# Layer two's phase of values: three tiles kept in DRAM during it, and the transposes for the queries issued beside the third value chunk

## The chip, the core and the metric

The kernel runs on one core of a Trainium2 chip. The metric is the device time of one execution in microseconds (us). Three runs of the kernel before took 2206.42, 2208.21 and 2209.02 us; their median is 2208.21 us. A separate execution was recorded by the hardware profiler: it took 2207.9 us on the device, and its trace spans 2206.1 us, so 1.8 us lie around the span. Every duration below comes from that one recorded execution.

## What is computed

A decoder trunk of two layers on 256 positions of width 2048, all in float32. Layer one mixes tokens by dilated attention and by attention into 256 memory tokens, and then runs a gated MLP with a short convolution. Layer two takes keys and values (`k_sh`, `v_sh`, 12 heads of 128) from the normed output of layer one, queries from its own norm, and mixes by stick-breaking attention and by 4-head attention into the memory tokens; the same kind of MLP follows.

```python
kv = _rmsnorm(x, g_kv) @ w_kv
k_sh, v_sh = jnp.split(kv, 2, axis=-1)
h = _rmsnorm(x, nrm[0])
q, qm = jnp.split(h @ w_in_b[lb], [SB_W], axis=-1)
o_sb = _stick_breaking(q.reshape(B, S, SB_HEADS, HEAD_DIM), k_sh, v_sh)
o_mem = _memory_attention(qm, mem, nrm[4], w_mem_kv[layer])   # mk, mv = rmsnorm(mem) @ w_mem_kv
x = _finish_layer(x, jnp.concatenate([o_sb.reshape(B, S, -1), o_mem], -1), ...)
```

## The kernel before

Nearly all of the time is matrix multiplication. Each float32 operand is split into a high part (`whi`, cast on ACT, line 629) and a low part (`wlo`, subtracted on DVE, line 630), and a product is made of three matmuls (`mm3`, line 127), or of a wider pair in `ws_tile` and `ws_beside`. Weights come in pieces of 1 MB or 768 KB into `raw`, which has three buffers, on SP's queue: the load of a piece waits until the piece three loads earlier has been split.

**The stage that the change touches.** After layer one's MLP, `run` goes through these steps, and the names are those of the profile:

- `mem_v(1)` has just made `mv`, the memory values (line 524 evacuates them); `mk`, the memory keys, was made long before, while layer one's output projection ran, and lies in its buffer through the whole MLP of layer one.
- `v_proj` (line 1159, `as_chunk`) makes `v2`, the third chunk of 512 values, from four pieces of weights. Each piece begins with `self.step()`, which runs whatever `later(units, fn)` has put there for that unit.
- `x_T` (lines 273 to 284) makes the transposed input of the queries: 32 transposes on PE (line 280) into PSUM, then 16 casts on ACT (269) and 16 subtractions on DVE (270) into `hq`.
- `qm_proj` makes the queries for the memory heads from `hq`, in four `ws_tile`s (lines 145 to 150).
- `values`, by way of `wide`, makes the other 1024 value columns in eight units. A unit multiplies seven half-size products instead of eight, over sums of the weights and sums of the input; beside it, `ws_beside` (lines 156 to 176) makes one tile of the keys. Everything in it is pinned, that is, it stays on each engine in the order in which the code writes it. The same routine runs in layer one (there beside tiles of queries and keys) and in the MLPs.

**What a unit u of `wide` loads and does.** `first_sums` brings `d` for unit u + 2: a 512 KB load on SP's queue (636), then an accumulating load of 512 KB on POOL's queue (637) into the same tile. `load` brings `raw` of unit u + 1 (668, 768 KB), and `ws_beside` the key weights of unit u + 1 (156, 1 MB). On SP's queue they stand in this order, so `raw` and the key weights wait behind `d`. DVE then makes the sums `e` from `d` and `raw` (674, 675), splits `raw` and the key weights, and splits `d` and `e` into the tiles `forms` (`x<-sh`, 630).

**The buffers.** `d` and `e` take buffers of the tag `sh`, of 512 KB each, of which there are 11. Through the phase of values eight are taken: `mk`, `mv`, `v2`, `qm` and the four places of `sums_of_h(hk, 4)`. Three are left, for two `d` and one `e`. So `d` of unit u + 2 goes where `d` of unit u lies, and its load waits for the split of that tile on DVE. In layer one's phase the sums of the input lie in a set of their own, and the waiting tiles are fewer: six `sh` buffers are left there.

Outside `wide` a scheduler sets each engine's order from the order of the code and from what is ready.

Of the kernel before, what the change touches and what calls it, by code (L numbers as in the profile page):

```python
# [10 lines left out]
F32 = mybir.dt.float32  # L11
# [6 lines left out]
P = 128  # L18
# [12 lines left out]
COL_G = {"a0": 0, "a2": 16, "a4": 32, "b0": 48, "b2": 64, "b4": 80, "kv": 96}  # L31
# [14 lines left out]
class Body:  # L46
# [49 lines left out]
    def pin(self, ins):  # L96
        return self.tc.keep_in_program_order(ins) if self.pinned else ins
# [291 lines left out]

    def dil_head(self, h, q, k, V, hi, lo, when):  # L390


        st = {}
        self.later(when[0], lambda: self.dil_scores(q, k, st))
        self.later(when[1], lambda: self.dil_turn(st))
        self.later(when[2], lambda: self.dil_out(h, V, st, hi, lo))

# [41 lines left out]

    def dil_out(self, h, V, st, hi, lo):  # L440
        nc = self.nc
        p0, p1 = st["p"]
        o = self.bank("s")
        hs = slice(h * E, (h + 1) * E)
        for g in range(3):
            nc.tensor.matmul(o[:, 0:P], V[g][:, 0, hs], p0[:, g, :], start=g == 0, stop=g == 2)
        for g in range(3):
            for kb in range(2):
                nc.tensor.matmul(o[:, P:S], V[g][:, kb, hs], p1[:, 2 * g + kb, :],
                                 start=g == 0 and kb == 0, stop=g == 2 and kb == 1)  # L450
        self.split_heads(o[:, :S], hi, lo)


    def sb_pair(self, j, q, k, V, outs, first):

        st = {}
        self.later(first, lambda: self.sb_scores(q, k, st))
        self.later(first + 3, lambda: self.sb_turn(st))
        self.later(first + 4, lambda: self.sb_out(j, V, st, outs))
# [85 lines left out]
    def out_proj(self, layer, src, lhs, each, filler=None):  # L545
# [39 lines left out]
        else:  # L585
            self.add_normed(ys, r[1], 1, each)

    def sums_of_h(self, h, ring=0):

        nc, pin = self.nc, self.pin
        if ring:
            places = [self.sh([P, 4, 2, P], F32R) for _ in range(ring)]
            room = lambda: self.sc([P, 2, S])
        else:
            whole = self.sb.tile([P, KT // 2, 4, 2, P], F32R, name="h1", tag="h1", bufs=1)
            places = [whole[:, i] for i in range(KT // 2)]
            room = self.pairtile  # L600
        s = lambda u: places[u % len(places)]

        def less(out, x, y):

            pin(nc.vector.scalar_tensor_tensor(out, x, -1.0, y, op0=ALU.mult, op1=ALU.subtract))

        def make(i):
            a, d = room(), room().rearrange("p a (b t) -> p (a b) t", b=2)
            hh = h[2][:, 2 * i:2 * i + 2, :, :].bitcast(F32)
            pin(nc.vector.tensor_add(a, hh[:, :, 0, :], hh[:, :, 1, :]))  # L610
            a1, a2 = a[:, :, 0:P], a[:, :, P:S]
            pin(nc.vector.tensor_sub(d[:, 0, :], a2[:, 1, :], a2[:, 0, :]))
            less(d[:, 1, :], d[:, 0, :], a1[:, 0, :])
            pin(nc.vector.tensor_sub(d[:, 2, :], a1[:, 0, :], a2[:, 0, :]))
            less(d[:, 3, :], d[:, 1, :], a1[:, 1, :])
            return lambda: self.split_heads(d, s(i)[:, :, 0, :], s(i)[:, :, 1, :])

        return s, make
# [391 lines left out]
    def run(self):  # L1010
        nc, a = self.nc, self.a
# [52 lines left out]
        mv = self.mem_v(0, before, 17)  # L1064
        h = self.hset("h2")
        mk = self.mem_k(0, lambda j: self.load_T(a["xT"], COL_G["a0"], h, j), 13)
# [24 lines left out]
        s, make = self.sums_of_h(h)  # L1091
        for i, at in enumerate((0, 1, 2, 2, 3)):
            self.later(at, lambda i=i: make(i)())
        ahead = []
        self.later(2, lambda: ahead.extend(self.first_sums(a["wv01_a"], u) for u in range(2)))
        v2 = self.v_proj(a["wv_a"][0], h)
        qm = self.qm_proj(a["wqm_a"], h, 1)

        forms = self.sb.tile([P, 4, 1024], F32R, name="x", tag="x", bufs=1)
# [15 lines left out]
        V = self.values(a["wv01_a"], ahead, h, s, forms, tile, self.rest_of(make)) + [v2]  # L1115
# [27 lines left out]
        hk = self.hset("h2")  # L1143
# [9 lines left out]
        mk, mv = res["mk"], res["mv"]  # L1153


        with self.tc.issue_after(self.last_hi.ins):
            self.r = self.x_rstd()
        self.later(3, spread)
        v2 = self.v_proj(a["wv_b"][0], hk)
        hq = self.hset("h1")  # L1160
        self.x_T(COL_G["b0"], hq)

        for t in range(2):
            self.later(0, lambda t=t: nc.gpsimd.dma_start(self.xout[t], self.x[:, t, :]))
        s, make = self.sums_of_h(hk, 4)
        for i in range(4):
            self.later(i, lambda i=i: make(i)())
        ahead = []
        self.later(2, lambda: ahead.extend(self.first_sums(a["wv01_b"], u) for u in range(2)))
        qm = self.qm_proj(a["wqm_b"], hq)  # L1170
        forms = self.sb.tile([P, 4, 1024], F32R, name="x", tag="x", bufs=1)
# [14 lines left out]
        def begin(i):  # L1186
            halves[i] = make(i)


        also = {0: lambda: begin(4), 1: lambda: halves[4](), 2: lambda: begin(5), 3: lambda: halves[5](),  # L1190
                4: lambda: (begin(6), halves[6]()), 5: lambda: begin(7), 6: lambda: halves[7]()}
        V = self.values(a["wv01_b"], ahead, hk, s, forms, tile, also) + [v2]
        self.x = sb.tile([P, 2, D], F32, name="x", tag="x", bufs=1)
        for t in range(2):
            self.later(8 + t, lambda t=t: nc.gpsimd.dma_start(self.x[:, t, :], self.xout[t]))
# [131 lines left out]
```

## Time and profile before

| | |
|---|---|
| median of three runs | 2208.21 us |
| profiled execution: time, span of the trace | 2207.9 us, 2206.1 us |
| mean granted TensorE clock over the span | 0.996 |
| instructions on PE, DVE, ACT, POOL | 10926, 2348, 1896, 195 |
| HBM read and written | 508.60 MB, 25.17 MB |
| phase of values in layer one, in the trace | from 98.7 to 182.5 us |
| `v_proj`, `qm_proj`, phase of values in layer two | from about 1114, 1139.6 and 1164.5 us, the last to 1266.0 us |

How to read the views that follow. A row of the timeline gives start and duration in us, engine, source line, operation, tile written and read, and in brackets the idle time before it with what ended it. A row of the waits names who waited for whom, with the total in us, how many times, and the longest. A row of the windows gives, for a stretch of the trace, its length and the busy time of PE, of its weight loads (PEld), DVE, ACT and POOL with the number of instructions, then the granted TensorE clock as a share of full speed, the share of the DMA engines that was busy, and GB/s. A row of one line's instructions gives their count, the least, median and longest duration in ns, and the start of the first and the last. SPq is SP's queue of DMA issues. The trace names the weights of all three value chunks `in_wv_b_dram`.

### The profile page before, as it was taken

To read this page: it belongs to the slowest core of one execution; us is meant where nothing else is said; L and a number is where in the kernel's file an instruction comes from. 1 tells how busy PE (TensorE), PEld (TensorE's weight loads), DVE (VectorE), ACT (ScalarE), POOL (GpSimd) and SP (SyncE) were. 2 spreads that over 40 slices of the span, in tenths; PEclk is the share of its full clock that TensorE was granted. 3 is DMA by queue.
4 is the path that set the end of the run, shared out by engine and by line. 5 is a ranking of instruction groups with operands and counts; after the bars stand their busy time and mean duration, and the time that the engine had idled before them with its cause. 6 is when DMAs were issued, how large, how long until landed. Compare 5 with 4: busy or idle time off the path is not lost.

```text
span 2206.1 us, 29290 instructions
## 1 busy us (share of the span) xinstructions
PE 2178.5 (99%) x10926; PEld 1830.9 (83%) x10926; DVE 1734.2 (79%) x2348; ACT 1327.1 (60%) x1896; POOL 173.7 (8%) x195
## 2 busy tenths in 40 slices
PE   9999999999999999999999899999999999999998
PEld 7888888888888888888887788878888888888886
DVE  7798867997887868788886868669977878687886
ACT  7566756666565666656574565456666656656563
POOL 0000001010101011010000000000001010110100
PEclk9999999999999999999999999999999999999999
DMA  9886557786979889797766754576969798797974
GB/s 351 256 260 242 173 187 248 225 267 227 291 229 286 258 247 289 214 294 264 260 213 186 240 190 155 180 238 214 276 221 289 238 281 262 235 294 227 284 242 180
DMA packets 109903, 535.69 MB, mean 243 GB/s; under 512 B 11072, under 2 KB 11456, under 8 KB 70720
## 3 DMA queue, kind: packets, MB, share of 16 engines
q1 hardware_dynamic: 74880, 445.72, 56.3%
q0 software_dynamic: 34880, 88.09, 19.9%
q8 instruction: 86, 1.41, 0.2%
q14 instruction: 57, 0.47, 0.1%
HBM read 508.60 MB, written 25.17 MB: 242 GB/s over the span
## 4 chain that ended last, share of the span: by engine, by line
PE 94%; DVE 2%; DMA 1%; issue 1%; ACT 0%; SPq 0%; POOL 0%; POOLq 0%; DVEq 0%; ACTq 0%
PE ps_g L128 39%; PE ps_s L163 24%; PE ps_s L128 11%; PE ps_g L145 10%; PE ps_g L146 5%; DVE wlo L630 1%; DMA raw<-in_wv_b_dram 1%; PE ps_s L922 1%; PE ps_g L148 1%; PE ps_s L280 1%; DMA raw<-in_wmv_dram 0%; PE ps_s L335 0%; PE ps_s L362 0%; DMA sh<-in_uw_dram 0%; DVE x L630 0%
## 5 line engine op out<-in xcount | busy, mean ns | idle before, releaser
L630 DVE TENSOR_TENSOR wlo<-raw,whi 128x1024 fp32r<-128x1024 f32 (+1 forms) x758 | 854.3, 1150 | 257.8 <-ACT whi L629 249.5
L629 ACT CAST whi<-raw 128x1024 fp32r<-128x1024 f32 (+1 forms) x758 | 741.5, 993 | 433.0 <-PE ps_g L128 174.9
L163 PE MATMUL ps_s<-h,whi 128*128 128x512 f32 x1536 | 555.9, 398 | 8.9 <-DVE qk L176 8.9
L128 PE MATMUL ps_g<-whi,sh 128*128 128x512 f32 x1488 | 464.2, 393 | 0.0
L163 PE MATMUL ps_s<-h,wlo 128*128 128x256 f32 x1536 | 416.9, 282 | 3.8 <-DVE wlo L630 3.8
L163 PEld LDWEIGHTS ps_s<-h,whi 128*128 128x128 f32 x1536 | 290.3, 189 | 73.0 <-ACT whi L629 11.0
L145 PE MATMUL ps_g<-h,whi 128*128 128x512 f32 x960 | 345.5, 401 | 1.1 <-DVE h L270 1.0
L128 PEld LDWEIGHTS ps_g<-whi,sh 128*128 128x128 f32 x1488 | 277.6, 188 | 57.4
L163 PEld LDWEIGHTS ps_s<-h,wlo 128*128 128x128 f32 x1536 | 291.3, 190 | 22.1 <-DVE wlo L630 6.2
L128 PE MATMUL ps_g<-wlo,sh 128*128 128x512 f32 x744 | 291.7, 392 | 0.0
L146 PE MATMUL ps_g<-h,wlo 128*128 128x256 f32 x1024 | 277.4, 281 | 0.0
L630 DVE TENSOR_TENSOR x<-sh,x 128x1024 fp32r<-128x1024 f32 x192 | 226.9, 1217 | 0.3 <-ACT x L629 0.3
L128 PE MATMUL ps_g<-whi,h 128*128 128x512 f32 x688 | 215.4, 394 | 1.5 <-ACT whi L629 1.5
L145 PEld LDWEIGHTS ps_g<-h,whi 128*128 128x128 f32 x960 | 180.5, 188 | 42.4 <-DVE h L270 1.8
L146 PEld LDWEIGHTS ps_g<-h,wlo 128*128 128x128 f32 x1024 | 193.6, 189 | 4.9
L629 ACT CAST x<-sh 128x1024 fp32r<-128x1024 f32 x192 | 192.6, 1045 | 1.5 <-DVE sh L675 1.5
L175 ACT COPY qk<-ps_s 128x256 f32<-128x256 f32 x96 | 35.8, 373 | 219.0 <-PE ps_s L163 219.0
L128 PEld LDWEIGHTS ps_g<-wlo,sh 128*128 128x128 f32 x744 | 139.7, 188 | 32.5
L128 PE MATMUL ps_s<-x,h 128*128 128x512 f32 x552 | 157.8, 394 | 0.0
L128 PE MATMUL ps_g<-x,h 128*128 128x512 f32 x528 | 151.4, 394 | 0.0
L637 POOL DMA_DIRECT2D sh<-in_uw_dram x80 | 98.6, 1232 | 662.6 <-DMA sh<-in_uw_dram 335.5
L128 PEld LDWEIGHTS ps_g<-whi,h 128*128 128x128 f32 x688 | 121.8, 188 | 27.7 <-ACT whi L629 2.4
(207 smaller groups left out, 2289.9 us busy)
## 6 DMA issues: line engine op xcount, KB each, us to landing
raw<-in_up_dram SPq DMA_DIRECT2D x96, 1024.0 KB, 6.7
raw<-in_dn_dram SPq DMA_DIRECT2D x88, 1024.0 KB, 5.6
raw<-in_uw_dram SPq DMA_DIRECT2D x80, 768.0 KB, 7.6
sh<-in_uw_dram SPq DMA_DIRECT2D x80, 512.0 KB, 8.1
sh<-in_uw_dram POOLq DMA_DIRECT2D x80, 512.0 KB, 10.5
raw<-in_wqk_a_dram SPq DMA_DIRECT2D x24, 1024.0 KB, 5.0
yout<-sh POOLq DMA_DIRECT2D x32, 512.0 KB, 8.6
raw<-in_wo_b_dram SPq DMA_DIRECT2D x16, 1024.0 KB, 4.8
```

What stands on the lines that cost most here:

```text
L128: mm = lambda *o, **k: self.pin(self.nc.tensor.matmul(*o, **k))
L145: mm(b, whi[:, ks], both, start=kt == 0, stop=False)
L146: mm(b[:, 0:S], wlo[:, ks], one, start=False, stop=False)
L148: mm(b, whi[:, ks], both, start=False, stop=True)
L163: mm = lambda *o, **k: self.pin(self.nc.tensor.matmul(*o, **k))
L175: self.pin(self.nc.scalar.copy(out, b[:, S:]))
L280: self.nc.tensor.transpose(b[:, k * S + t * P:k * S + (t + 1) * P], self.x[:, t, kt * P:(kt + 1) * P], self.ident)
L629: high = self.pin(self.nc.scalar.copy(hi, of))
L630: low = self.pin(self.nc.vector.tensor_sub(lo, of, hi.bitcast(F32)))
L637: self.nc.gpsimd.dma_start(d.rearrange("p (a n) -> p a n", a=2), src[u][:, 1536:].unsqueeze(1).to_broadcast([P, 2, 512]), accum_op=ALU.add)
L922: nc.tensor.transpose(b[:, j * S + t * P:j * S + (t + 1) * P], of[t][:, f:f + P], self.ident)
```

## The change

`mk`, `mv` and `v2` are each written to DRAM as soon as they exist, which frees their buffers, and are loaded back into new buffers after the phase of values. The four quarters of `x_T` for the queries are put into the four steps of `v_proj` instead of after it.

```diff
+    def set_aside(self, tile, name):
+
+        there = self.outside.tile([P, 1024], F32, name=name)
+        self.nc.gpsimd.dma_start(there, tile.rearrange("p a n -> p (a n)"))
+
+        def back():
+            new = self.sh([P, tile.shape[1], tile.shape[2]])
+            self.nc.gpsimd.dma_start(new.rearrange("p a n -> p (a n)"), there)
+            return new
+
+        return back
...
         self.later(3, spread)
+        hq = self.hset("h1")
+        for c in range(4):
+            self.later(c, lambda c=c: self.x_T(COL_G["b0"], hq, [c]))
         v2 = self.v_proj(a["wv_b"][0], hk)
-        hq = self.hset("h1")
-        self.x_T(COL_G["b0"], hq)

         for t in range(2):
             self.later(0, lambda t=t: nc.gpsimd.dma_start(self.xout[t], self.x[:, t, :]))
+
+        kept = [self.set_aside(t, k) for t, k in ((mk, "mk"), (mv, "mv"), (v2, "v2"))]
...
-        V = self.values(a["wv01_b"], ahead, hk, s, forms, tile, also) + [v2]
+        V = self.values(a["wv01_b"], ahead, hk, s, forms, tile, also)
+        mk, mv, v2 = (back() for back in kept)
+        V.append(v2)
```

Lines below the new function stand 12 higher in the changed kernel: 636 is 648 there, 637 is 649, 668 is 680.

**SP's queue in the phase of values.** The rows are the loads for `d`, `raw` and the key weights of three units in a row, with the names of the semaphores that each waits for: DMAHW and DMASW count landed loads of SP's and POOL's queue, DVE_49 the progress of DVE. Before:

```order
L636 DMA sh<-in_wv_b_dram 128x1024 [waits DMAHW5_49,DMASW2_49,DVE_49]
L668 DMA raw<-in_wv_b_dram 128x1536 [waits DMAHW3_49]
L156 DMA raw<-in_wk_b_dram 128x2048 [waits DMAHW7_49,DVE_49]
L636 DMA sh<-in_wv_b_dram 128x1024 [waits DMAHW6_49,DMASW3_49,DVE_49]
L668 DMA raw<-in_wv_b_dram 128x1536 [waits DMAHW4_49]
L156 DMA raw<-in_wk_b_dram 128x2048 [waits DMAHW1_49]
L636 DMA sh<-in_wv_b_dram 128x1024 [waits DMAHW0_49,DMASW4_49,DVE_49]
L668 DMA raw<-in_wv_b_dram 128x1536 [waits DMAHW2_49]
L156 DMA raw<-in_wk_b_dram 128x2048 [waits DMAHW4_49]
```

The same place in the changed kernel:

```order
L648 DMA sh<-in_wv_b_dram 128x1024 [waits DMASW0_49]
L680 DMA raw<-in_wv_b_dram 128x1536 [waits DMAHW3_49,DVE_49]
L156 DMA raw<-in_wk_b_dram 128x2048 [waits DMAHW7_49,DVE_49]
L648 DMA sh<-in_wv_b_dram 128x1024 [waits DMASW4_49]
L680 DMA raw<-in_wv_b_dram 128x1536 [waits DMAHW4_49,DVE_49]
L156 DMA raw<-in_wk_b_dram 128x2048 [waits DMAHW5_49,DMAHW1_49,DVE_49]
L648 DMA sh<-in_wv_b_dram 128x1024 [waits DMAHW6_49,DMASW7_49,DMASW3_49]
L680 DMA raw<-in_wv_b_dram 128x1536 [waits DMAHW2_49,DVE_49]
L156 DMA raw<-in_wk_b_dram 128x2048 [waits DMAHW4_49,DMAHW0_49,DVE_49]
```

The order of the loads is the same; the wait for DVE has left the loads of `d` and stands now at those of `raw` and of the key weights, where it is the split of what lay in that `raw` buffer before.

**POOL's queue around the phase of values.** First the stores of `x`, then the accumulating loads for `d`, then the loads of `x` and of the gains. Before:

```order
L1164 DMA xout<-x 128x2048 x2
L239 TENSOR_TENSOR small<-small,mhalf 128x2
L637 DMA sh<-in_wv_b_dram 128x2x512 x8
L1195 DMA x<-xout 128x2048 x2
L532 DMA sc<-in_gb_dram 128x512 x4
```

In the changed kernel (`v_10062` is the copy of `v2` in DRAM):

```order
L1177 DMA xout<-x 128x2048 x2
L591 DMA mv<-sh 128x1024
L239 TENSOR_TENSOR small<-small,mhalf 128x2
L591 DMA v_10062<-sh 128x1024
L649 DMA sh<-in_wv_b_dram 128x2x512 x8
L1212 DMA x<-xout 128x2048
L595 DMA sh<-mk 128x1024
L595 DMA sh<-mv 128x1024
L595 DMA sh<-v_10062 128x1024
L1212 DMA x<-xout 128x2048
L532 DMA sc<-in_gb_dram 128x512 x4
```

Five transfers were put in here, the loads back between the two of `x`. The sixth, the store of `mk`, stands in layer one's MLP, behind the first two accumulating loads there.

**PE at the end of `v_proj`.** `h_2796` is the input of `v_proj`, the rows of lines 145 and 146 belong to `qm_proj`, line 280 is the transposes. Before, its last rows and the start of `qm_proj`:

```order
L128 MATMUL ps_g<-wlo,h_2796 128x512
L280 MATMUL ps_s<-ident,x 128x128 x16
L145 MATMUL ps_g<-h_9985,whi 128x512
L146 MATMUL ps_g<-h_9985,wlo 128x256
L145 MATMUL ps_g<-h_9985,whi 128x512
L146 MATMUL ps_g<-h_9985,wlo 128x256
L280 MATMUL ps_s<-ident,x 128x128 x12
```

In the changed kernel, where the last of its four pieces begins:

```order
L128 MATMUL ps_g<-wlo,h_2796 128x512
L251 MATMUL ps_s<-ident,small 128x128 x2
L280 MATMUL ps_s<-ident,x 128x128 x8
L128 MATMUL ps_g<-whi,h_2796 128x512 x2
L128 MATMUL ps_g<-wlo,h_2796 128x512
```

Eight transposes stand ahead of each of the four pieces of `v_proj`, and none between `v_proj` and the end of `qm_proj`.

## The prediction

> **What bounds the kernel now.** I read the page's list of engines and its chain first.
>
> ```profile
> span 2206.1 us, 29290 instructions
> PE 2178.5 (99%) x10926; PEld 1830.9 (83%) x10926; DVE 1734.2 (79%) x2348; ACT 1327.1 (60%) x1896; POOL 173.7 (8%) x195
> PE 94%; DVE 2%; DMA 1%; issue 1%; ACT 0%; SPq 0%; POOL 0%; POOLq 0%; DVEq 0%; ACTq 0%
> ```
>
> TensorE sets the end. A change that leaves its matmuls as they are, as this one does, can win only where PE stands still or its clock is lowered. PE's waits say where it stands still.
>
> ```profile
> PE ps_s L163 <- DVE qk L176: 8.9, 4, 4.0
> PE ps_s L163 <- DVE wlo L630: 3.8, 7, 0.6
> PE ps_g L145 <- DVE h L270: 1.0, 1, 1.0
> PE ps_s L280 <- DVE h L270: 0.3, 1, 0.3
> ```
>
> The two largest waits are at line 163, the seven-product matmuls of `wide`, and the other two are in the transposes for the queries. `wide` makes the value phase in both layers, so layer one is a ready measure: the windows give its phase first and layer two's second, then two stretches of the latter, and below them stand the line's starts.
>
> ```profile
> 98.70:182.50 83.80, 83.80 (x425) 70.57 (x424) 75.64 (x101) 52.20 (x68) 6.01 (x5) 1.00 0.79 250
> 1164.50:1266.00 101.50, 89.96 (x426) 73.28 (x425) 74.45 (x100) 48.74 (x62) 6.40 (x6) 0.95 0.69 216
> 1190.00:1200.00 10.00, 10.00 (x47) 8.43 (x46) 4.79 (x7) 2.34 (x3) 1.20 (x1) 0.86 0.65 219
> 1220.00:1230.00 10.00, 10.00 (x45) 8.44 (x44) 4.86 (x7) 2.36 (x3) 1.20 (x1) 0.82 0.65 221
> L163 PE MATMUL ps_s<-h,whi x128: 389/395/418, 98.7 to 179.6; 128*128 128x512 f32 x128
> L163 PE MATMUL ps_s<-h,whi x128: 387/396/764, 1164.5 to 1262.9; 128*128 128x512 f32 x128
> ```
>
> The work is the same (425 and 426 matmuls, 75.64 and 74.45 us of DVE), yet from the first matmul of line 163 to its last, layer two takes 98.4 us against 80.9, with PE idle for 101.5 − 89.96 = 11.5 us and the clock at 0.95 instead of 1.00. One turn of the loop, on the timeline:
>
> ```profile
> 1177.75 2.35 DVE L630 TENSOR_TENSOR x<-sh,x 128x1024 fp32r<-128x1024 f32 x2
> 1179.00 0.33 SPq L636 DMA_DIRECT2D sh<-in_wv_b_dram  x1
> 1179.38 0.42 SPq L668 DMA_DIRECT2D raw<-in_wv_b_dram  x1
> 1179.85 0.42 SPq L156 DMA_DIRECT2D raw<-in_wk_b_dram  x1
> 1184.72 0.69 DVE L674 TENSOR_TENSOR sh<-sh,raw 128x512 f32<-128x512 f32 x1 [4.62 <-DMA raw<-in_wv_b_dram]
> 1188.36 0.47 PE L163 MATMUL ps_s<-h,whi 128*128 128x512 f32 x1 [2.64 <-DVE qk L176]
> ```
>
> The load of `d` (636) goes out when DVE has split the tile that lies in its buffer. `raw` and the key weights leave 0.4 and 0.9 us later, though their buffers were free: they stand behind it. `raw` lands at 1184.72, DVE has waited 4.62 us, and PE then waits 2.64 us. The waits of SP and DVE over the phase show that this is the loop:
>
> ```profile
> SPq L636 <- DVE x L630: 60.6, 5, 15.4
> DVE sh L674 <- DMA raw<-in_wv_b_dram: 20.7, 4, 5.8
> ```
>
> **The change part by part.**
>
> *Three tiles leave the buffers.* Of 11, six remain for `d` and `e` instead of three, as in layer one. The load of `d` loses its wait for DVE. `raw` and the key weights get one of their own, for the split of what lay in their buffer; behind the load of `raw` stand on SP the key weights, and then `d` of the next unit. When would that be late? Unit 0's `raw` was split here:
>
> ```profile
> 1166.21 0.68 DVE L630 TENSOR_TENSOR wlo<-raw,whi 128x512 fp32r<-128x512 f32 x1
> DMA to landing us min/median/max: 4.5/6.3/9.3
> SPq L668 <- DVE wlo L630: 26.0, 7, 4.9
> ```
>
> So the load of 1179.38 could have left at about 1167. With the median of its line (second row) it lands at 1173.3, and DVE needs it at 1180.1, when its splits end (1177.75 + 2.35): 6.8 us of cover. The last row is layer one's phase, where this very wait costs SP 26.0 us and PE none. I therefore take layer one's length: 98.4 − 80.9 = **−17.5 us**. Of it 11.5 is idleness, 0.05 × 101.5 = 5.1 the lowered clock, and 0.9 the rest.
>
> [...]
>
> *A heavy unit gives a little back.* In unit 4 the code puts two portions of sums beside one unit. DVE's units start at their first row of line 674:
>
> ```profile
> 1229.08 0.69 DVE L674 TENSOR_TENSOR sh<-sh,raw 128x512 f32<-128x512 f32 x1 [5.11 <-DMA raw<-in_wv_b_dram]
> 1240.45 0.68 DVE L674 TENSOR_TENSOR sh<-sh,raw 128x512 f32<-128x512 f32 x1
> 1250.65 0.68 DVE L674 TENSOR_TENSOR sh<-sh,raw 128x512 f32<-128x512 f32 x1
> ```
>
> One unit takes 11.4 us, the next 10.2, without a wait inside; PE's unit is 83.80 / 8 = 10.5. Once nothing waits for loads, DVE is 0.9 late in the heavy one. Layer one shows no such wait but carries other work there. Bounds: 0, if the unit before hides it, and 4 × 0.9 = 3.6 if every second unit is as heavy. The nearest row is the one heavy unit: **+0.9**.
>
> *The transposes go into `v_proj`.* Their 32 matmuls, 16 casts and 16 subtractions stay; what goes is that PE stands alone with them:
>
> ```profile
> 1136.66 1.91 PE L280 MATMUL ps_s<-ident,x 128*128 128x128 f32 x16
> 1139.04 4.29 DVE L270 SCALAR_TENSOR_TENSOR h<-ps_s,cols,h 128x256 fp32r<-128x256 f32 x10
> 1140.84 1.50 PE L280 MATMUL ps_s<-ident,x 128*128 128x128 f32 x12 [0.30 <-DVE h L270]
> 1105.00:1139.00 34.00, 33.57 (x174) 27.99 (x172) 26.71 (x52) 26.03 (x51) 0.72 (x1) 1.00 0.58 208
> ```
>
> The waits of 1.0 and 0.3 us quoted above end: **−1.3**. DVE takes its 16 × 0.43 = 6.9 us to an earlier place, where it idles 34.00 − 26.71 = 7.3 us, and the stretch grows by PE's 32 transposes (3.5 us), so DVE has cover for all of it: 0. If none of it were hidden, it would cost 6.9. Such DVE work there also stands ahead of the split of the next piece of weights, for which PE would wait; that is in the 6.9.
>
> *Three stores on POOL.* Each needs an issue on POOL's queue, which holds up what is behind it until its tile is evacuated.
>
> ```profile
> 1114.71 0.74 ACT L524 ACTIVATE sh<-ps_g,rm 128x512 f32<-128x512 f32 x1
> 1125.44 0.72 POOL L239 TENSOR_TENSOR small<-small,mhalf 128x2 f32<-128x2 f32 x1 [24.70 <-DVE small L237]
> 1137.59 0.68 ACT L524 ACTIVATE sh<-ps_g,small 128x512 f32<-128x512 f32 x1
> 1145.71 2.53 POOL L637 DMA_DIRECT2D sh<-in_wv_b_dram  x2 [19.55 <-DMA sh<-in_wv_b_dram]
> 382.02 0.72 POOL L239 TENSOR_TENSOR small<-small,mhalf 128x2 f32<-128x2 f32 x1 [19.79 <-DVE small L237]
> ```
>
> `mv` is there at 1115.5, POOL's next row begins at 1125.44 after 24.7 us of idleness; `v2` is there at 1138.3, or with the transposes ahead of it at 1141.8, and the next row is 1145.71; behind the store of `mk` stands the row of 382.02, after 19.8 idle. Idleness of 24.7, 19.6 and 19.8 us covers a store's issue: 0. Were it not hidden, one issue is 0.57 (half of the pair at 1266.42 below), three 1.7.
>
> *Three loads on POOL.* They go out between the two of `x`, when the phase's last matmul is done, and `mk` is needed first, by line 335.
>
> ```profile
> 1266.42 1.13 POOL L1195 DMA_DIRECT2D x<-xout  x2 [29.38 <-DVE sh L734]
> DMA to landing us min/median/max: 5.1/8.0/10.9
> 1277.24 1.02 PE L335 MATMUL ps_s<-sh 128*128 128x256 f32 x4
> ```
>
> Today 2 MB of `x` are in 10.9 us after the second issue (1267.0), 11.5 after 1266.4: 182 GB/s on this queue, with the weights' loads beside it. `x[0]` and `mk` are 1.5 MB, so 8.6 us by that pace, and line 335 comes 10.8 us after the issue: 2.2 us of cover, **0**. It is the thinnest cover here. If the queue's five transfers (3.5 MB) shared its pace evenly, `mk` would land with the last, after 20.1 us: +9.3.
>
> [...]
>
> ```profile
> 1266.00:1268.00 2.00, 2.00 (x13) 1.73 (x12) 1.97 (x4) 0.00 (x0) 1.13 (x2) 1.00 0.32 61
> ```
>
> Both loads of `x` were issued in 1.13 us with DVE busy for 1.97 of 2.00. [...]
>
> **The sum.** −17.5 + 0.9 − 1.3 + 0 = −17.9 us. The profiled execution took 2207.9 us (2206.1 of span and 1.8 around it), 0.3 from the median of the runs, which I take as noise: 2207.9 − 17.9 = **2190.0 us**.
>
> **The rivals.**
>
> 1. *`mk` comes late.* PE stands at line 335 until it lands. For it: five transfers on one queue, 2.2 us of cover. Against it: the first of two transfers landed after 5.1 us, the second after 10.9, so a queue serves them in order. Up to +9.3 gives 2191 to 2199.
> 2. *DVE becomes the bound of the phase.* For it: 11.4 against 10.5 us in the heavy unit. Against it: 75.64 us of DVE in layer one's 83.80 without idleness. With four heavy units 3 × 0.9 = 2.7 more, 2192.7; with all eight 2196.3.
> 3. *The lowered clock isn't from the stalls.* The gain is then 11.5 + 1.3 = 12.8: 2195.1. Against it stands layer one's clock of 1.00 at the same work.
> 4. *The loads don't come free*, since something else holds them, and the loop stays: only the 1.3 is won, 2206.6. Against it: in the order of the changed kernel the waits for DVE have left line 648.
> 5. *Slower*: the loads of `mk` collide with the weights so hard that PE stands longer than all that is won. The point: 17.9 + 4.4 = 22.3 us of PE standing at line 335, so `mk` 33.1 us after the issue, 47 GB/s for 1.5 MB where 182 was measured. That gives over 2212.
>
> **How the numbers follow.** A measurement of this kernel can tell about 0.2% from no change, which is 4.4 us: faster is below 2203.8. Forecast 0.76, rival 1 0.10, rival 2 0.06, rivals 3 and 4 0.03 each, rival 5 0.02. The low end, 2186, is the forecast without the 0.9, with 1.3 more should the clock's restarts at the transposes go as well, and with the 1.8 by which the runs of before went under their median. The high end, 2199, takes in rivals 1 to 3; the 6.9 at the transposes (2196.9) and the 1.7 of the stores (2191.7) lie within it. Left out are rivals 4 and 5, and about 0.1 for a miss of the forecast itself. Faster is the forecast with rivals 1 to 3, 0.95; same is rival 4, 0.03; slower is rival 5, 0.02.
>
> **What the profile after would show.** *Right:* line 163 takes 81 to 82 us from first to last start, the phase's clock is 1.00; SP's wait at 648 for the splits of `x` is gone and stands at 680 and 156 for `wlo`; DVE's wait at 686 for `raw` is gone; PE waits nowhere for line 270 of the transposes, and not at line 335. *Wrong:* DVE still waits at 686 for `raw` (rival 4); PE waits in the phase for `wlo` or `qk` by 0.9 a unit and more (rival 2); a clock below 1.00 without idleness (rival 3); PE at line 335 waits for the load of `mk` (rivals 1 and 5). The prediction falls with its largest term if layer two's phase keeps a limit that layer one's doesn't have.

## The result, and the profile after

The changed kernel took 2192.22 us (median of four runs, 2191.80 to 2193.01), beside 2207.58 us for the kernel before, timed with it (median of four, 2206.42 to 2209.02). The ratio is 0.9931 with a 95% interval of 0.9913 to 0.9948: some 15 us faster, between 11.5 and 19.2. The prediction was 2190.0 us within 2186 to 2199. So the time lies in the range, 2.2 us above the forecast. By themselves 2.2 us are little beside the spread of the medians (further down the same kernel is only 12.9 us under the kernel before), so what follows is read from the traces, stage by stage.

The page of the profiled execution after:

```profile
span 2190.5 us, 29303 instructions
PE 2172.2 (99%) x10926; PEld 1828.2 (83%) x10926; DVE 1734.1 (79%) x2348; ACT 1327.4 (61%) x1896; POOL 177.3 (8%) x201
```

The work is as before (10926 matmuls, 1734.1 us of DVE), POOL has six DMAs more, and the span is 15.6 us shorter. PE's waits between 1090 and 1290 us, then the windows of layer one's phase of values, of layer two's, and of the latter's first 9.3 us:

```profile
PE ps_s L163 <- DVE wlo L642: 2.0, 2, 1.6
PE ps_s L163 <- ACT whi L641: 0.5, 1, 0.5
```

```profile
98.60:182.40 83.80, 83.80 (x425) 70.59 (x425) 75.69 (x101) 52.26 (x68) 5.99 (x5) 1.00 0.79 251
1162.70:1251.20 88.50, 86.49 (x426) 72.18 (x427) 80.54 (x108) 52.32 (x66) 5.99 (x5) 0.98 0.78 248
1162.70:1172.00 9.30, 7.75 (x31) 6.28 (x32) 9.23 (x13) 5.67 (x8) 0.00 (x0) 0.82 0.63 177
```

And the group of line 163 in layer two, with its first and last start:

```profile
L163 PE MATMUL ps_s<-h,whi x128: 387/398/628, 1162.7 to 1247.9; 128*128 128x512 f32 x128
```

The phase went from 98.4 to 85.2 us, not to the 81 to 82 that layer one's phase promised. PE's idleness in it fell from 11.5 to 88.50 − 86.49 = 2.0 us, and most of what is left stands in the first 9.3 us: 1.55 us of idleness, and a clock of 0.82, which is another 0.18 × 9.3 = 1.7 us. The waits of SP and DVE in the phase say that the loop itself is gone:

```profile
SPq L680 <- DVE wlo L642: 20.8, 7, 3.8
DVE sh L686 <- DMA sh<-in_wv_b_dram: 6.9, 1, 6.9
```

SP no longer waits for the split of `x` at line 648; it waits at 680 for the split of what lay in `raw`, as forecast, and DVE never waits for `raw`. A new wait stands at 686: once, at the phase's start, DVE waits 6.9 us for the first `d`. The timeline of that start, picked from the rows of ACT, SP, POOL, DVE and PE:

```profile
1139.50 1.05 ACT L641 CAST whi<-raw 128x1024 fp32r<-128x1024 f32 x1 [0.32 <-PE ps_g L128]
1141.96 0.33 SPq L680 DMA_DIRECT2D raw<-in_wv_b_dram  x1
1142.38 1.04 SPq L648 DMA_DIRECT2D sh<-in_wv_b_dram  x2
1148.87 0.33 SPq L156 DMA_DIRECT2D raw<-in_wk_b_dram  x1
1150.36 2.50 POOL L649 DMA_DIRECT2D sh<-in_wv_b_dram  x2 [8.35 <-DMA sh<-in_wv_b_dram]
1160.48 0.69 DVE L686 TENSOR_TENSOR sh<-sh,raw 128x512 f32<-128x512 f32 x1 [6.93 <-DMA sh<-in_wv_b_dram]
1162.65 0.50 PE L163 MATMUL ps_s<-h,whi 128*128 128x512 f32 x1 [0.54 <-ACT whi L641]
1164.71 0.38 PE L163 MATMUL ps_s<-h,wlo 128*128 128x256 f32 x1 [1.55 <-DVE wlo L642]
```

Read it from below. PE's two waits come from DVE's late sums, these from the accumulating load (649), issued at 1150.36 and landed 10.1 us later. That one had to wait for the plain load of `d`, which stands on SP's queue behind the first `raw` (680, at 1141.96). In the kernel before, whose rows run 0.8 us behind these, the same three were at 1139.14 (`raw`), 1145.71 (accumulating load) and 1156.05 (sums, with no wait):

```profile
1139.14 0.33 SPq L668 DMA_DIRECT2D raw<-in_wv_b_dram  x1
1152.14 0.33 SPq L156 DMA_DIRECT2D raw<-in_wk_b_dram  x1
1156.05 0.68 DVE L674 TENSOR_TENSOR sh<-sh,raw 128x512 f32<-128x512 f32 x1
```

The first row of the changed kernel says why `raw` is late: it waits for a split whose cast on ACT waited for matmuls of line 128, the third value chunk.

The profile's difference by stage, between the same rows of POOL: up to the row at 1092.01 (1091.24 after) 0.8 us, from there to the first load of `x` (1266.42 before, 1251.36 after) 14.3, behind it 0.5. The first part is most likely not the change's doing: it grows evenly through layer one's MLP. That stretch (POOL's line 239 from 382.02 to 1089.42 us before) takes 707.4 us before, 706.7 in this profile and 707.1 to 708.0 in the others below, whose MLP is the same but for the store of `mk`. So the change gave 14.3 us in its stage.

### The profile page after: what moved, and what is told of

It is laid out like the page before. It is cut to its first block, busy times and chain, and to the rows that moved or that the text cites. A ratio compares the mean times of both kernels' runs of the same rounds, so it can differ in the third digit from the quotient of the medians.

```text
span 2190.5 us, 29303 instructions
## 1 busy us (share of the span) xinstructions
PE 2172.2 (99%) x10926; PEld 1828.2 (83%) x10926; DVE 1734.1 (79%) x2348; ACT 1327.4 (61%) x1896; POOL 177.3 (8%) x201
## 4 chain that ended last, share of the span: by engine, by line
PE 96%; DMA 1%; DVE 1%; issue 1%; ACT 0%; SPq 0%; POOL 0%; POOLq 0%; DVEq 0%; ACTq 0%
PE ps_g L128 40%; PE ps_s L163 25%; PE ps_s L128 12%; PE ps_g L145 10%; PE ps_g L146 5%; DMA sh<-in_wv_b_dram 1%; PE ps_s L934 1%; PE ps_g L148 1%; PE ps_s L280 1%; DVE wlo L642 0%; DMA raw<-in_wmv_dram 0%; PE ps_s L335 0%; PE ps_s L362 0%; DMA sh<-in_uw_dram 0%; PE ps_s L467 0%
```

## The experiments

Each was timed beside the kernel before, in 4 to 11 executions; rows with the same time of the kernel before were timed together. To compare them without what varies elsewhere, each profile gives the **stage**: from the last row of POOL's line 239 ahead of the stores of `x` (at 1092.01 us before) to the first load of `x` behind the phase.

| kernel | median, before beside it (us) | ratio, 95% interval | stage (us) | line 163, first to last (us) |
|---|---|---|---|---|
| before (its profile) | | | 174.4 | 98.4 |
| changed (its profile) | 2192.22, 2207.58 | 0.9931, 0.9913 to 0.9948 | 160.1 | 85.2 |
| transposes_only | 2209.20, 2209.18 | 1.0000, 0.9991 to 1.0009 | 175.1 | 100.8 |
| aside_only | 2192.87, 2209.18 | 0.9926, 0.9914 to 0.9939 | 157.5 | 81.5 |
| mk_only | 2194.65, 2209.18 | 0.9934, 0.9922 to 0.9947 | 159.9 | 85.0 |
| early_dv | 2189.92, 2209.18 | 0.9913, 0.9899 to 0.9926 | 155.8 | 81.6 |
| after_again | 2195.90, 2208.76 | 0.9937, 0.9924 to 0.9951 | 160.4 | 85.1 |
| x_first | 2199.24, 2208.76 | 0.9953, 0.9941 to 0.9966 | 159.3 | 84.6 |
| early_old_T | 2191.26, 2208.76 | 0.9921, 0.9909 to 0.9934 | 157.7 | 81.8 |
| mk_early | 2190.28, 2208.76 | 0.9915, 0.9902 to 0.9929 | 156.0 | 81.7 |
| T_first | 2191.59, 2207.38 | 0.9928, 0.9914 to 0.9941 | 160.2 | 85.3 |

The two rows of POOL of the changed kernel, as an example of how a stage is read (1251.36 − 1091.24 = 160.1):

```profile
1091.24 0.92 POOL L239 TENSOR_TENSOR small<-small,mhalf 128x1 f32<-128x1 f32 x1 [1.65 <-DVE small L237]
1251.36 0.58 POOL L1212 DMA_DIRECT2D x<-xout  x1 [35.42 <-DVE sh L746]
```

**One part of the change alone.** `transposes_only` is the kernel before with

```diff
+        hq = self.hset("h1")
+        for c in range(4):
+            self.later(c, lambda c=c: self.x_T(COL_G["b0"], hq, [c]))
         v2 = self.v_proj(a["wv_b"][0], hk)
-        hq = self.hset("h1")
-        self.x_T(COL_G["b0"], hq)
```

> Only the transposes move into the third value chunk, nothing is set aside. Theory: the loop through the buffers stays, so PE idles some 11 us in the phase as before; at most 1.3 us is won, and up to 2.8 us may be lost since the first loads leave later and the loop hangs on the loads: 2206 to 2210 us. Rival: the transposes carry a part of the gain themselves, by letting the phase begin earlier: under 2204 us.

`aside_only` is the changed kernel with this edit taken back.

> The three tiles are set aside, the transposes stay behind the third value chunk. Theory: the buffers carry the whole gain of the phase, and the changed kernel gives 3.8 us back at the start of the phase (2.1 us of PE idle, 1.7 us of lowered clock), because the transposes' work on DVE lets the first loads of the phase out 2.8 us later. Here these loads leave early again and the phase starts without a wait, while PE waits 1.3 us in the transposes: 2192.2 + 1.3 - 3.8 = 2189.7 us, line 163 from first to last start 81 to 82 us. Rival: the start is late because of the setting aside itself (its stores and the freed loads collide with the first loads); then the phase starts late here too, 2193 to 2194 us.

The transposes alone won nothing: 0.0 us, and the stage is 0.7 us longer. In the profile of transposes_only PE's two waits of 1.3 us are gone, and in their place PE waits 3.2 us at the phase's start, the third row here; the loop stays, as the others show:

```profile
PE ps_s L163 <- DVE qk L176: 5.6, 3, 3.6
PE ps_s L163 <- DVE wlo L630: 3.4, 6, 0.6
PE ps_s L163 <- ACT whi L629: 3.2, 1, 3.2
DVE sh L674 <- DMA raw<-in_wv_b_dram: 20.2, 4, 5.4
```

The buffers alone won the whole: in aside_only line 163 takes 81.5 us, 16.9 less than before, and of its waits of PE between 1090 and 1290 us only the second, 0.5 us, lies in the phase:

```profile
PE ps_g L145 <- DVE h L270: 1.0, 1, 1.0
PE ps_s L163 <- DVE wlo L642: 0.5, 1, 0.5
PE ps_s L280 <- DVE h L270: 0.3, 1, 0.3
```

So, with the tiles set aside, the moved transposes cost 160.1 − 157.5 = 2.6 us of the stage. The expected 2189.7 us was missed by the median (2192.87, beside a kernel before that was 1.6 us slower than the one beside the changed kernel). In the profiled execution, which took 2193.45, 2 us were lost at the place of the last section; whether the median's execution lost them there is not shown.

**How many buffers.** `mk_only` is the changed kernel with

```diff
-        kept = [self.set_aside(t, k) for t, k in ((mk, "mk"), (mv, "mv"), (v2, "v2"))]
+        kept = [self.set_aside(t, k) for t, k in ((mk, "mk"),)]
-        mk, mv, v2 = (back() for back in kept)
+        mk, = (back() for back in kept)
```

> Only the memory keys are set aside, so four buffers are left for d and e instead of six; the transposes are moved as in the changed kernel. In its order the load of d then waits for a split that lies a whole unit earlier than in the kernel before. Theory: one unit earlier is enough, since raw then lands some 4 us before its sums; the phase is as in the changed kernel, 2191 to 2193 us. Rival 1: each buffer is worth a third of the gain, 2202 us. Rival 2: the loop stays as long as any load of d waits for DVE, 2204 us or more.

The stage is 159.9 us, as with three tiles (160.1), and PE's waits in it are the same 2.1 and 0.4 us at line 163. The median is 14.5 us under the kernel before; 2194.65 is outside the expected 2191 to 2193, by little more than that kernel's own 1.6 us. Both rivals fall: four buffers carry the whole gain. In mk_only the loads of `d` still wait for DVE, 27.5 us where the kernel before waited 60.6, but for the split of a sum that lies one unit earlier:

```profile
SPq L648 <- DVE x L642: 27.5, 4, 8.1
```

**The start of the phase.** `early_dv` is the changed kernel with the first two loads of `d` put beside the last piece of the third value chunk:

```diff
+        ahead = []
+        self.later(3, lambda: ahead.extend(self.first_sums(a["wv01_b"], u) for u in range(2)))
         v2 = self.v_proj(a["wv_b"][0], hk)
...
-        ahead = []
-        self.later(2, lambda: ahead.extend(self.first_sums(a["wv01_b"], u) for u in range(2)))
```

> The changed kernel, with the first two loads of d issued beside the last piece of the third value chunk, ahead of the weights of the memory queries. Theory: the start of the phase is late because the accumulating load of the first d lands late (it leaves 4.6 us later than in the kernel before and takes 10.1 us instead of 7.5); with that load out of the way the 3.8 us at the start go: 2188.4 us, and PE waits at line 163 only in the heavy unit. Rival: the weights of the memory queries come later by the 2 MB put ahead of them and PE waits there, 2190 us or more; or the start hangs on raw or on DVE instead, 2192 us.

The stage fell by 4.3 us to 155.8, and the median is 19.3 us under the kernel before, as expected (2188.4 is 19.2 under the 2207.58 beside the changed kernel). The 7.5 us of the expectation is the kernel before's second accumulating load; its first took 6.1. In early_dv the group of line 163 has no slow matmul any more (the longest takes 403 ns, not 628), and PE waits there for 0.5 us in all:

```profile
L163 PE MATMUL ps_s<-h,whi x128: 387/395/403, 1163.6 to 1245.2; 128*128 128x512 f32 x128
```

**What makes the first loads late.** The expectation for aside_only had put it down to DVE, which has the transposes' subtractions to do. `T_first` has the transposes in the first two steps of the chunk, so that DVE is done with them early:

```diff
-            self.later(c, lambda c=c: self.x_T(COL_G["b0"], hq, [c]))
+            self.later(c // 2, lambda c=c: self.x_T(COL_G["b0"], hq, [c]))
```

> The changed kernel with the four quarters of the transposes in the first two steps of the third value chunk instead of one in each of four. Theory: raw of the phase's first unit waits for a split whose cast on ACT waits for a buffer that the last matmuls of the third value chunk hand back; PE's 32 transposes stand ahead of these wherever they are put in the chunk, so the load leaves as late as in the changed kernel, d lands late and PE waits some 2 us at the first unit: 13 to 15 us under the kernel before. Rival: the load is late because DVE has the transposes' subtractions to do at the chunk's end; with these done earlier it leaves some 3 us sooner, the phase starts without a wait, and the kernel is 17 to 19 us under the kernel before.

The stage stayed at 160.2 us. In the timeline of T_first DVE's last subtraction of the transposes lies ahead of 1130 us, the first row here, and the load is as late as ever:

```profile
1128.88 0.48 DVE L270 SCALAR_TENSOR_TENSOR h<-ps_s,cols,h 128x256 fp32r<-128x256 f32 x1
1140.13 1.06 ACT L641 CAST whi<-raw 128x1024 fp32r<-128x1024 f32 x1 [0.29 <-PE ps_g L128]
1141.40 1.22 DVE L642 TENSOR_TENSOR wlo<-raw,whi 128x1024 fp32r<-128x1024 f32 x1
1142.64 0.33 SPq L680 DMA_DIRECT2D raw<-in_wv_b_dram  x1
```

The cast waits for PE's line 128, the chunk's matmuls; the split and the load follow at once. It is PE's order that counts: 3.5 us of transposes stand ahead of the matmuls that hand back `whi`. The median (15.8 us under the kernel before) is 0.8 beyond what I had expected, but the waits at the first unit (2.0 and 0.4 us) are those of the changed kernel.

**The transposes once `d` is early, and the fewest transfers.** `early_old_T` is early_dv with the transposes back behind the chunk; `mk_early` is early_dv with only `mk` set aside.

> The three tiles set aside and the first two loads of d early, but the transposes behind the third value chunk. Theory: with d early the transposes cost only PE's 1.3 us of waits: 17 to 18 us under the kernel before, 1 to 2 us over the kernel with the early loads and the moved transposes (which was 19.3 under). Rival: the waits in the transposes are made up elsewhere, or the start of the phase hangs on the place of the transposes in another way; then no difference to it, or 3 us and more.

> Only the memory keys set aside, the first two loads of d early, the transposes moved. Theory: four buffers carry the whole gain of the phase, and the transfers of mv and v2 cost nothing: 19 to 20 us under the kernel before, the same as with all three set aside. Rival: with d held for two units early, four buffers are too few, the loads of d wait for DVE again, and 2 us or more of the gain go.

early_old_T: 17.5 us under the kernel before, stage 157.7, so the move of the transposes wins 157.7 − 155.8 = 1.9 us, once nothing at the phase's start hangs on it. mk_early: 18.5 us under, half a microsecond short of the 19 to 20 expected, and stage 156.0, the same as early_dv: the stores of `mv` and `v2` and their loads cost nothing that can be seen, and bring nothing either.

**The reload of `mk`.** `x_first` is the changed kernel with both loads of `x` ahead of the loads of the three tiles:

```diff
-        mk, mv, v2 = (back() for back in kept)
-        V.append(v2)
         self.x = sb.tile([P, 2, D], F32, name="x", tag="x", bufs=1)
         for t in range(2):
-            self.later(8 + t, lambda t=t: nc.gpsimd.dma_start(self.x[:, t, :], self.xout[t]))
+            nc.gpsimd.dma_start(self.x[:, t, :], self.xout[t])
+        mk, mv, v2 = (back() for back in kept)
+        V.append(v2)
```

> The changed kernel with both loads of x ahead of the loads of mk, mv and v2 on POOL's queue. Theory: the queue serves its transfers in order; x then takes its 11.5 us from the issue as in the kernel before and mk half a MB more, 14.1 us, while line 335 comes after 10.8: PE waits 3.3 us there, and with a lowered clock behind it up to 1.7 us more is lost: 3 to 5 us over the changed kernel. Rival 1: the transfers share the queue's pace evenly, so their order does not matter and the time is that of the changed kernel. Rival 2: nothing waits for mk before its cover of 0.7 us and some more is used up because line 335 can be passed by other matmuls: under 1 us over.

`after_again` is the changed kernel itself, timed beside it.

> The changed kernel once more, beside the others of this call: 15 to 16 us under the kernel before, as first measured.

First the changed kernel's issue of the load of `mk` on the timeline, with the group of line 335 behind it:

```profile
1251.93 0.56 POOL L595 DMA_DIRECT2D sh<-mk  x1
```

```profile
L335 PE MATMUL ps_s<-sh x16: 378/379/382, 1262.2 to 1286.6; 128*128 128x256 f32 x16
```

The load of `mk` took 9.4 us to land, the first of the three loads back that this row of the DMA view spans:

```profile
DMA to landing us min/median/max: 9.4/10.2/12.5
```

So `mk` is in at 1261.3, and line 335 begins at 1262.2: 0.9 us in time. Then x_first, its timeline and the window behind the wait:

```profile
1253.63 0.53 POOL L595 DMA_DIRECT2D sh<-mk  x1 [0.23 <-issue]
1266.82 1.10 PE L335 MATMUL ps_s<-sh 128*128 128x256 f32 x4 [3.57 <-DMA sh<-mk]
```

```profile
1266.80:1276.80 10.00, 9.98 (x49) 8.83 (x50) 4.38 (x7) 3.60 (x7) 0.00 (x0) 0.83 0.42 154
```

PE waits 3.57 us where 3.3 were expected, and the 10 us behind it run at 0.83 of the clock, another 1.7. From the first load of `x` to POOL's next row of line 239 x_first takes 207.5 us, where before, changed and after_again take 202.2: 5.3 us, at the wait's place. In x_first the two loads of `x` landed at 1257.5 and 1263.9 and `mk`, issued 0.8 us after the second, at 1266.7: the queue served its transfers in order. The medians differ by 3.3 us only, since after_again lost 2.0 us elsewhere (last section); it was 12.9 us under the kernel before, not the 15 to 16 expected.

x_first shows something else at the phase's start. It has nearly the waits of the changed kernel there (0.35 and 1.56 us for 0.54 and 1.55), but its clock stays at 1.00, as the row for its first 9.3 us says:

```profile
1164.20:1173.50 9.30, 7.22 (x34) 5.36 (x35) 9.23 (x13) 5.57 (x8) 0.00 (x0) 1.00 0.67 183
```

PE then waits another 0.5 us for DVE, and the stage is 0.8 us shorter than in the changed kernel, 1.1 shorter than in after_again. So the 1.7 us of lowered clock at that place do not follow from the stop each time, and without them no more than about 1 us was won.

## Why the prediction was right, and where 2.2 us went

- **The phase (−17.5 + 0.9).** Right in mechanism and, apart from the start, in size. With nothing else touched (aside_only) line 163 takes 16.9 us less, against 16.6 forecast; PE's idleness and the lowered clock went together, as the four kernels with a stage of 156 to 158 us show, which wait 0.4 to 0.5 us in the phase at a mean clock of 1.00. The changed kernel got 13.2 of it.
- **The lowered clock (rival 3).** It falls. Between 1090 and 1290 us the clock of the changed kernel is below 1.00 only in the window behind PE's stop at the phase's start (0.82), and in x_first it is 0.83 behind the stop at line 335 and 1.00 in the two windows up to its end (1250 to 1266.8 us). In the kernel before, the windows at 0.86 and 0.82 are full of matmuls and lie behind stalls, and layer one's phase without idleness is at 1.00. So in these windows a lowered clock came only behind a stop; but a stop was not always followed by one. The stops of 0.54 and 1.55 us at the phase's start, with one matmul between them, were followed by 0.82 in the changed kernel, those of 0.35 and 1.56 us by 1.00 in x_first. What decides between the two is not shown.
- **The heavy unit (+0.9).** PE waits 0.4 to 0.5 us, once, behind the heavy unit, in the kernels whose phase is otherwise free. Rival 2 falls with it.
- **The transposes (−1.3).** This is the step that failed: −1.3 was forecast, and beside the freed buffers the move cost 2.6. I wrote that DVE "has cover for all of it: 0", and looked for the cost on PE and DVE only. The waits of 1.3 us did go; but the loads of the phase's first unit hang on the last matmuls of the third value chunk, through the buffers of `whi`, and 3.5 us of transposes were put ahead of these. `raw` left 2.8 us later (3.6 with the 0.8 by which this profile runs ahead), and the accumulating load took 10.1 us to land instead of 6.1. These are the first of the transfers that the next rows span, the first row from the kernel before, the second from the changed one:

```profile
DMA to landing us min/median/max: 6.1/7.5/8.0
DMA to landing us min/median/max: 8.7/10.1/11.6
```

In the changed kernel the load of the key weights leaves 1.5 us ahead of it; in transposes_only, mk_only and T_first the two leave within 1 us of each other, and it took 9.5 to 11.4 us. In the kernel before and in aside_only the key weights leave at 1152.14 and 1152.20, after it has landed, and it took 6.1. That the two loads hold each other up fits all six, but is not shown: no run moves the key weights alone. The cover between these loads and the phase's start was gone. Alone the move costs 0.7 us of the stage, beside the freed buffers 2.6: the term was off by 3.9 us, and it ate part of the first one. The bound of +6.9 that I kept for it held, though for another reason. The 1.3 us that the low end of the range allowed for restarts of the clock at the transposes had no row behind it: the clock is 1.00 there in the kernel before (1139 to 1145 us).

- **The stores (0).** Right: mk_only and mk_early, without those of `mv` and `v2`, have the same stages as their counterparts (159.9 us for 160.1, 156.0 for 155.8).
- **The reload (0).** Right, but by less than I worked out. `x[0]` and `mk` took 1261.3 − 1251.4 = 10.0 us, not 8.6 (157 GB/s instead of 182), and the cover was 0.9 us instead of 2.2. x_first shows what rival 1 would have cost beyond it: the wait, and half as much again in clock. With DVE busy for 4.93 of 5 us (1251 to 1256 us, all of its rows TENSOR_TENSOR) POOL issued the five loads in 2.9 us, 0.57 each, the pace of the two loads of `x` in the kernel before.

The sum: −16.6 forecast for the phase with the heavy unit and −1.3 for the transposes make −17.9; the stage gave −14.3, so it fell 3.6 us short, and 1.3 came from pace elsewhere in the span. That these 1.3 us bring the time to within 2.2 us of the forecast is luck.

Not tried: spreading the heavy unit's sums over its neighbours, and issuing the load of `mk` ahead of `x[0]`.

**The better version.** early_dv and mk_early are both faster than the changed kernel: 0.9913 and 0.9915 of the kernel before, and 4.2 to 4.3 us shorter in the stage. Timed together, mk_early took 2189.76 to 2190.92 us and the changed kernel (after_again) 2193.96 to 2196.42. mk_early does it with two transfers of 512 KB instead of six.

## What to carry to other kernels

Where a queue issues in order, ask of each waiting load what stands behind it: one buffer more, which moves the wait one turn earlier, gave here as much as three (a stage of 159.9 us beside 160.1). Before work is moved ahead on the engine that sets the end, list the loads whose buffers are handed back by what it is put in front of; a wait of 1.3 us was removed and 3.9 us were paid at a place some 25 us later. A stop of the tensor engine can cost more than its own length: behind the stop of 3.57 us in x_first the clock was 0.83 for 10 us, another 1.7 us, but behind a stop of 2.03 us it fell in one execution (after_again, to 0.75 and 0.57) and stayed at 1.00 in another (changed).

## What the runs showed that I had not expected

A stop of PE at one place of layer two costs 2 us more in some executions of the same code. Behind the rows of POOL at 1459.06 (changed) and 1459.95 (after_again), PE waits 2.03 us for the rows of `x` in both, then 0.85 and 0.30 us in the changed kernel and 0.56 in after_again. The stop begins alike, but the clock behind it differs. The windows of the changed kernel and then of after_again, 5 us each:

```profile
1459.00:1464.00 5.00, 2.50 (x16) 1.88 (x16) 4.91 (x10) 2.37 (x7) 2.49 (x5) 1.00 1.03 290
1464.00:1469.00 5.00, 4.88 (x34) 4.55 (x35) 4.48 (x11) 4.17 (x11) 0.00 (x0) 1.00 1.05 288
```

```profile
1460.00:1465.00 5.00, 3.08 (x16) 2.47 (x17) 4.91 (x10) 2.48 (x7) 2.45 (x5) 0.75 1.03 294
1465.00:1470.00 5.00, 5.00 (x24) 4.73 (x23) 3.53 (x9) 2.86 (x7) 0.00 (x0) 0.57 1.07 295
```

The same work takes 19.4 us to the next row of line 239 in the changed kernel (1459.06 to 1478.41) and 21.4 in after_again (1459.95 to 1481.34). In the profiles of transposes_only, mk_only, early_dv, mk_early, early_old_T and x_first it is 19.3 or 19.4, in those of T_first and aside_only 21.5 and 21.4, in that of the kernel before 19.6, whose clock falls there too (0.74 from 1477 to 1482 us). What decides whether the clock falls behind this stop is not shown: no run here moves the stop on purpose. For the reader it means that two executions of one kernel can differ by 2 us at one place, and that a stage read from the trace tells apart what the medians of five executions do not. after_again's five lie in two groups, two near 2194.0 at a mean clock of 0.998 and three near 2196.2 at 0.997, and 0.001 of the clock is 2.2 us over the span; only one of the five was profiled, so that all three lost them at this place is not shown.
